# Raw weight loads with the gate sum's unit third, and the gate sum added by VectorE in pairs 3, 5 and 7

## The chip, the core and the metric

The kernel runs on one core of a Trainium2 chip. A core has a matrix engine (PE, with its weight loads shown as PEld), VectorE (DVE), ScalarE (ACT), GpSimd (POOL) and SyncE (SP), which run their own instruction streams and wait for one another by semaphores. SP and POOL here mostly issue DMAs; sixteen DMA engines carry them. The metric is the device time of one execution in microseconds (us), as a median of runs.

## The reference

A decoder trunk of two layers over 512 tokens with model width 1024, in float32. Each layer is a feed-forward block, a token mixing and a second feed-forward block; a last norm follows.

```python
def swiglu(h, w_gate, w_up, w_down):
    return (jax.nn.silu(h @ w_gate) * (h @ w_up)) @ w_down

for l in range(DEPTH):                      # DEPTH = 2, D_MODEL = 1024, D_FF = 2816
    x = x + 0.5 * swiglu(rms_norm(x, ffn1_norm[l]), ffn1_wg[l], ffn1_wu[l], ffn1_wd[l])
    h = rms_norm(x, mix_norm[l])
    z = h @ w_in[l]                         # q | k | v | conv_B | conv_C | conv_h
    ...                                     # sliding-window attention and a short convolution
    x = x + jnp.concatenate([attn_out, conv_out], axis=-1) @ w_out[l]
    x = x + 0.5 * swiglu(rms_norm(x, ffn2_norm[l]), ffn2_wg[l], ffn2_wu[l], ffn2_wd[l])
return rms_norm(x, final_norm)
```

Nearly all the work is in the weight products: four feed-forward blocks with gate, up and down weights, and two mixings with their input and output weights.

## The kernel before, in words

**Precision.** Each weight tile of 128 x 1024 is loaded raw (512 KB) and split in two: ScalarE casts it to a high part wh, VectorE subtracts to get the rest, wl (function `split`, line 228). PE then makes three products per piece: wh with the high part of the activations, wh with their low part, wl with the high part. Activations are split the same way. wh and wl have three buffers each, so a split can run at most about two groups ahead of PE; `take_split` asks for the split two places ahead (`SPLIT_AHEAD`).

**Seven products instead of eight.** Most weights are multiplied by a Winograd scheme on 2 x 2 quarters of the weights. With a11, a12, a21, a22 as quarters, the weight forms used are, in this order (`FORMS`): a11, a12, s2 = a11 + s1, s3 = a21 + a11, s1 = a21 + a22, a22, s4 = a12 + s2, signs left to the activations' side. This is called a seven here. In the gate and up weights, quarter rows are the two weights (gate quarters a11 and a12, up quarters a21 and a22) and s3 is the sum that the change calls the gate sum. Each form comes in two halves h of one 128 x 1024 tile, so a seven has 14 groups, and PE takes them one after another: seven steps of 24 products (line 837, or 822 in the mixing).

**Where sevens occur.** A feed-forward block runs its stages in the order of `INNER`: a plain stage and a down stage, then five pairs of gate and up blocks (`("w", b)` with b = 1, 3, 5, 7, 9), then two down-projection sevens (`("s", 1)` and `("s", 5)`), then a rest. The last block of the kernel ends with a stage of its own (`("e", 5)`) in place of the second down-projection seven. Each mixing has one seven for its output weights. That makes twenty sevens of pairs, four of `("s", 1)`, three of `("s", 5)` and two of the mixing. In the traces, tiles of the down-projection sevens end in `_s`, of the mixing in `_m`, of the last stage in `_e`.

**Raw loads.** `plan` lists the loads as units, two (h = 0 and 1) for each of five raw tiles of a seven: a11; s1, loaded as a21 with a22 accumulated onto it; a12; s3, loaded as a21 with a11 accumulated onto it; a22. `need_raw` issues the first load of a unit on SP's queue (line 210 for its DMA) and the second, where there is one, as an accumulating DMA on POOL's queue (line 223). An accumulating DMA waits until the plain load has landed. The raw tiles share eight buffers, so a load starts when an earlier tile has been released; SP's queue stands in the order of the units.

**In-place sums.** a11's tile becomes s2 when VectorE adds s1 to it (line 269), after a11 itself has been split. a12's tile becomes s4 when that s2 is added to it, once a12 has been split: by VectorE (line 291) or, in the sevens marked "share", by an accumulating DMA (line 289). a11 and s3 are released at form s3, s1 at its own form, a22 at its own, a12 at s4.

**What sets the order of work.** The instruction order on each engine comes from a planner that walks the program with its own estimates of durations: it takes the earliest instruction in program order that is ready by its clock. The order is fixed at build time; at run time each engine waits in that order. `tc.issue_after` adds edges by hand: in "share" sevens the s2 addition is placed behind the split just before it (`state["rest"]`). `last` in `need_split` and `LOAD_AHEAD` only say how far ahead in program order loads are requested.

Of the kernel before, what the change touches and what calls it, by code (L numbers as in the profile page):

```python
# [75 lines left out]
def trunk_kernel(  # L76
# [23 lines left out]
    nc = tc.nc  # L100
# [92 lines left out]
    units = []  # L193
    order = []
    raw_of, split_of = {}, {}
# [4 lines left out]
    def add_unit(*unit):  # L200
        units.append(unit)
        return len(units) - 1
# [24 lines left out]
    def split(hi, lo, raw, eng=nc.vector):  # L227
        return nc.scalar.copy(hi, raw), eng.tensor_sub(lo, raw, f32(hi))  # L228

    def split_far(hi, lo, raw):  # L230

        nc.scalar.activation(lo, raw, AF.Copy, scale=-1.0)
        nc.scalar.copy(hi, raw)
        return nc.gpsimd.dma_start(out=f32(lo), in_=raw, accum_op=ALU.add)

    def need_split(g):
        while state["split"] <= min(g, len(order) - 1):
            n = state["split"]
            u, what = order[n]
            far = what == "far"  # L240
            if what in (None, "far"):
                need_raw(u if far else max(u, min(u + LOAD_AHEAD, state["hold"] or len(units))))
                raw = raw_of.pop(u)
            elif isinstance(what, tuple) and what[0] == "end":

                _, what, h = what
                at = {"a11": 2, "s2": 2, "s3": 3, "s1": 3, "a12": 4, "a22": 5, "s4": 5}[what]
                need_raw(u + 3 * at + h + LOAD_AHEAD)
                raws = {name: u + 3 * i + h for i, name in enumerate(END_LOADS)}
                if what == "s2":  # L250
                    with tc.issue_after(state["rest"]):
                        nc.vector.tensor_add(raw_of[raws["a11"]], raw_of[raws["a11"]], raw_of[raws["s1"]])
                raw = raw_of[raws["a11" if what in ("s2", "s4") else what]]
            elif isinstance(what, tuple):

                what, h, how = what
                far = how == "far"
                last = {"a11": 0, "a12": 4, "s2": 2, "s3": 6, "s1": 2, "a22": 8, "s4": 4}[what]
                need_raw(u + h if far else u + max(last, 4) + h + LOAD_AHEAD)
                a11, s1, a12, s3, a22 = (raw_of.get(u + 2 * i + h) for i in range(5))  # L260
                if what == "s2":

                    late = state["late"] if h else None
                    if not state["late"] and how == "share":
                        late = state["rest"]
                    if how == "behind":
                        late = state["mark"]
                    with tc.issue_after(late) if late else nullcontext():
                        nc.vector.tensor_add(a11, a11, s1)  # L269
                raw = {"a11": a11, "a12": a12, "s2": a11, "s3": s3, "s1": s1, "a22": a22, "s4": a12}[what]  # L270
            shape = list(raw.shape)
            hi = wpool.tile(shape, F32R, tag="wh", bufs=3, name=f"wh_{n}")
            lo = wpool.tile(shape, F32R, tag="wl", bufs=3, name=f"wl_{n}")
            if far:
                sent = split_far(hi, lo, raw)
            else:
                state["cast"], state["rest"] = (i.ins for i in split(hi, lo, raw))
                if isinstance(order[n][1], tuple) and order[n][1][2] == "mark":
                    state["mark"] = state["rest"]
            if isinstance(order[n][1], tuple) and order[n][1][0] == "end":  # L280
                if what == "a12":
                    nc.gpsimd.dma_start(out=raw_of[raws["a11"]], in_=raw, accum_op=ALU.add)
                if what in ("s3", "s1", "a12", "a22"):
                    del raw_of[raws[what]]
                if what == "s4":
                    del raw_of[raws["a11"]]
            elif isinstance(order[n][1], tuple):
                if what == "s3" and how == "share":
                    nc.gpsimd.dma_start(out=a12, in_=a11, accum_op=ALU.add)
                elif what == "s3":  # L290
                    nc.vector.tensor_add(a12, a12, a11)
                done = {"s3": (0, 3), "s1": (1,), "a22": (4,), "s4": (2,)}.get(what, ())
                for i in done:
                    del raw_of[u + 2 * i + h]
            split_of[n] = (hi, lo)
            state["split"] += 1
            if far:

                with tc.issue_after(sent.ins):
                    need_raw(u + LOAD_AHEAD + (4 + h if isinstance(order[n][1], tuple) else 0))  # L300
# [26 lines left out]
    def abreast(kc):  # L327

        return max(1, KC // kc) if kc in (2, 4) else 1
# [34 lines left out]
    def plan():  # L364
        def cols(src, k0, kc, n, how=None, last=False):
            wide = abreast(kc)
            for b in halves_of(n, wide, last):
                order.append((add_unit((src, k0, kc, b * P, wide * P)), how))

        def plain(wg, wu, b):  # L370
            for w in (wg, wu):
                for j in range(2):
                    order.append((add_unit((w, 0, KC, (2 * b + j) * P, P)), None))

        def seven(at, how):


            u = len(units)
            for what in (((0, 0),), ((1, 0), (1, 1)), ((0, 1),), ((1, 0), (0, 0)), ((1, 1),)):
                for h in range(2):  # L380
                    add_unit(*(at(o, j, h) for o, j in what))
            order.extend((u, (what, h, how(what, h))) for what in FORMS for h in range(2))

        def ffn(wg, wu, wd, stages, near=False):
            for what, b in stages:
                how = "far" if b == (0,) and not near else None
                if what == "p":
                    plain(wg, wu, b)
                if what == "w":
                    seven(  # L390
                        lambda o, j, h: ((wg, wu)[o], KC // 2 * j + 2 * h, 2, 2 * b * P, S),
                        lambda what, h: "far"
                        if (b, what, h) == (1, "a11", 0)
                        else {("a12", 0): "mark", ("s2", 1): "behind"}.get((what, h))
                        if near and b == 3
                        else None,
                    )
                if what == "s":
                    seven(
                        lambda o, j, h: (wd, 2 * b + KC // 2 * j + 2 * h, 2, o * S, S),  # L400
                        lambda what, h: None if (b, what) == (1, "s3") else "share",
                    )
                if what == "d":
                    cols(wd, 2 * b[0], 2 * len(b), KC, how, len(b) == 2)
                    if len(b) == 2:
                        closing.append(len(units) - 1)
                if what == "e":
                    u = len(units)
                    roomy.update(range(u, u + 3))
                    for form_ in END_LOADS:  # L410
                        ojs = {"s1": ((1, 0), (1, 1)), "s3": ((1, 0), (0, 0))}
                        for i in range(3):
                            add_unit(
                                *(
                                    (wd, 2 * b + (KC + 2 * j if i == 2 else KC // 2 * j + 2 * i), 2, o * S, S)
                                    for o, j in ojs.get(form_, ((0, int(form_ == "a12")) if form_ != "a22" else (1, 1),))
                                )
                            )
                    order.extend((u, ("end", what, i)) for what in END_FORMS for i in range(3))

        for l in range(DEPTH):
            ffn(ffn1_wg[l], ffn1_wu[l], ffn1_wd[l], INNER, l == 0)
            for c in MIX_COLS:
                for j in range(2):
                    order.append((add_unit((w_in[l], 0, KC, (2 * c + j) * P, P)), None))
            seven(
                lambda o, j, h: (w_out[l], KC // 2 * j + 2 * h, 2, o * S, S),
                lambda what, h: "share",
            )
            ffn(ffn2_wg[l], ffn2_wu[l], ffn2_wd[l], INNER if l + 1 < DEPTH else LAST)  # L430
# [1349 lines left out]
```

## Time and profile before

| | |
|---|---|
| median of 3 runs | 1626.28 us (1625.93 to 1626.74) |
| profiled execution | 1626.23 us |
| its span, first to last instruction | 1624.4 us |
| PE busy | 1615.6 us, 7571 products |
| VectorE busy | 1376.8 us |
| ScalarE busy | 1177.8 us |
| POOL busy | 216.4 us |
| accumulating loads from wg, wu, wd, w_out | 40, 40, 34, 8 of 512 KB |
| granted PE clock | 1.0 throughout |

The profiled execution is one run of the program; its time is larger than its span by what lies outside the first and last instruction. Busy time of PE is counted from pipelined products whose ends are modelled, so the pace of product starts says more than the busy share. In the trace's rows a start and a duration in us come first, then engine, line, operation, tiles (written <- read), and in brackets the idle time before the instruction and what ended it. Rows of a queue (SPq) are issues of DMAs.

### The profile page before, as it was taken

Reading aid. Unit: us, or ns where it says so; the run is one execution under the profiler, and the core shown is the slowest. Engines: PE = TensorE matmul, PEld = TensorE weight load, DVE = VectorE, ACT = ScalarE, POOL = GpSimd, SP = SyncE. Lnnn points to the kernel's source line nnn. Section 1 sums busy time; section 2 is a strip of 40 time slices with the busy share of each in tenths; the row PEclk is TensorE's granted clock in tenths of the full one; section 3 lists DMA queues with packets and bytes.
Section 4 is the critical chain, followed back from the end, with each engine's and each line's share of the span. In section 5 each row is a group of like instructions: output and inputs, shape, how many; then the busy total and the mean of one; then the engine's idle time right before and its main releaser. Section 6 shows DMA issues by size and latency. Waiting matters only on the chain.

```text
span 1624.4 us, 21158 instructions
## 1 busy us (share of the span) xinstructions
PE 1615.6 (99%) x7571; PEld 1348.7 (83%) x7571; DVE 1376.8 (85%) x1788; ACT 1177.8 (73%) x1511; POOL 216.4 (13%) x191
## 2 busy tenths in 40 slices
PE   9999999999999999999999999999999999999998
PEld 7888888888898888888888888888888988888887
DVE  7978798988899877798998777989688998678997
ACT  6667777857766677778865777788586767878665
POOL 1211111001211111111011111110012111111121
PEclk9999999999999999999999999999999999999999
DMA  9999999823597699999767999998136978999892
GB/s 268 214 232 208 228 208 212 238 60 78 139 228 178 174 224 217 217 211 227 220 143 183 224 214 227 213 220 216 45 91 156 233 149 220 227 220 220 245 228 72
DMA packets 306030, 313.92 MB, mean 193 GB/s; under 512 B 125500, under 2 KB 188548, under 8 KB 305924
## 3 DMA queue, kind: packets, MB, share of 16 engines
q1 hardware_dynamic: 265412, 230.90, 50.0%
q0 software_dynamic: 40048, 81.27, 29.2%
q8 instruction: 59, 0.97, 0.2%
q10 hardware_dynamic: 464, 0.40, 0.1%
q14 instruction: 47, 0.39, 0.1%
HBM read 264.29 MB, written 2.10 MB: 164 GB/s over the span
## 4 chain that ended last, share of the span: by engine, by line
PE 96%; DVE 2%; ACT 1%; DMA 1%; issue 0%; SPq 0%; ACTq 0%; DVEq 0%
PE x L837 27%; PE y L837 13%; PE x_s L837 9%; PE acc L318 7%; PE w L837 7%; PE acc L319 7%; PE acc L321 7%; PE y_s L837 5%; PE x_m L822 3%; PE w_s L837 3%; PE y_m L822 1%; PE y_e L837 1%; PE x_e L837 1%; PE acc L699 1%; PE w_m L822 1%; DVE wl L228 1%
## 5 line engine op out<-in xcount | busy, mean ns | idle before, releaser
L228 DVE TENSOR_TENSOR wl<-raw,wh 128x1024 fp32r<-128x1024 f32 (+1 forms) x494 | 599.1, 1221 | 162.4 <-ACT wh L228 161.0
L228 ACT CAST wh<-raw 128x1024 fp32r<-128x1024 f32 (+1 forms) x494 | 513.7, 1043 | 303.9 <-PE x L837 92.9
L318 PE MATMUL acc<-xh,wh 128*128 128x512 f32 x392 | 153.3, 393 | 0.5 <-ACT wh L228 0.5
L319 PE MATMUL acc<-xl,wh 128*128 128x512 f32 x392 | 153.1, 391 | 0.0
L321 PE MATMUL acc<-xh,wl 128*128 128x512 f32 x384 | 149.6, 390 | 0.0
L223 POOL DMA_DIRECT2D raw<-in_ffn_wu_dram x40 | 50.6, 1277 | 380.6 <-DMA raw<-in_ffn_wu_dram 200.4
L318 PEld LDWEIGHTS acc<-xh,wh 128*128 128x128 f32 x392 | 73.8, 188 | 15.2 <-ACT wh L228 0.6
L319 PEld LDWEIGHTS acc<-xl,wh 128*128 128x128 f32 x392 | 73.7, 188 | 14.4
L321 PEld LDWEIGHTS acc<-xh,wl 128*128 128x128 f32 x384 | 72.1, 188 | 15.2
L223 POOL DMA_DIRECT2D raw<-in_ffn_wd_dram x34 | 41.0, 1218 | 272.9 <-DMA raw<-in_ffn_wd_dram 166.7
L223 POOL DMA_DIRECT2D raw<-in_ffn_wg_dram x40 | 49.0, 1232 | 205.2 <-DMA raw<-in_ffn_wu_dram 105.0
L269 DVE TENSOR_TENSOR raw<-raw,raw 128x1024 f32<-128x1024 f32 x58 | 70.5, 1220 | 3.2 <-DMA raw<-in_ffn_wu_dram 2.0
L1101 ACT COPY raw_a<-turned 128x1024 uint16<-128x1024 uint16 x48 | 63.5, 1357 | 0.0
L837 PE MATMUL x<-wl,ft1h 128*128 128x512 f32 x160 | 62.4, 390 | 0.0
L837 PE MATMUL w<-wh,fb21h 128*128 128x512 f32 x160 | 62.3, 390 | 0.0
L837 PE MATMUL y<-wh,ft3h 128*128 128x512 f32 x160 | 62.3, 390 | 0.0
L837 PE MATMUL x<-wl,ft2h 128*128 128x512 f32 x160 | 62.3, 389 | 0.0
L837 PE MATMUL x<-wh,ft1h 128*128 128x512 f32 x160 | 62.3, 389 | 0.0
L837 PE MATMUL x<-wh,ft2h 128*128 128x512 f32 x160 | 62.3, 389 | 0.0
L837 PE MATMUL x<-wh,ft1l 128*128 128x512 f32 x160 | 62.3, 389 | 0.0
L837 PE MATMUL x<-wh,ft2l 128*128 128x512 f32 x160 | 62.2, 389 | 0.0
L837 PE MATMUL w<-wh,fb21l 128*128 128x512 f32 x160 | 62.2, 389 | 0.0
(517 smaller groups left out, 4546.6 us busy)
## 6 DMA issues: line engine op xcount, KB each, us to landing
raw<-in_ffn_wu_dram SPq DMA_DIRECT2D x127, 512.0 KB, 5.4
raw<-in_ffn_wd_dram SPq DMA_DIRECT2D x105, 512.0 KB, 5.6
raw<-in_ffn_wg_dram SPq DMA_DIRECT2D x86, 512.0 KB, 5.2
raw<-in_ffn_wu_dram POOLq DMA_DIRECT2D x40, 512.0 KB, 9.0
raw<-in_ffn_wg_dram POOLq DMA_DIRECT2D x40, 512.0 KB, 6.2
raw<-in_w_in_dram SPq DMA_DIRECT2D x36, 512.0 KB, 4.0
raw<-in_ffn_wd_dram POOLq DMA_DIRECT2D x34, 512.0 KB, 8.4
raw<-in_w_out_dram SPq DMA_DIRECT2D x20, 512.0 KB, 4.1
```

The costliest lines, as they stand in the source:

```text
L223: nc.gpsimd.dma_start(out=r, in_=rows_of(*more), accum_op=ALU.add)
L228: return nc.scalar.copy(hi, raw), eng.tensor_sub(lo, raw, f32(hi))
L269: nc.vector.tensor_add(a11, a11, s1)
L318: nc.tensor.matmul(acc, hi[:, k, :], rhs[k][0], start=k == first, stop=False)
L319: nc.tensor.matmul(acc, hi[:, k, :], rhs[k][1], start=False, stop=False)
L321: nc.tensor.matmul(acc, lo[:, k, :], rhs[k][0], start=False, stop=k == last)
L699: nc.tensor.matmul(opening[n], (lo if part == "w" else hi)[:, k, :], xl if part == "x" else xh, start=n not in begun, stop=k == KC - 1 and ...
L822: nc.tensor.matmul(accs[c // 2][:, c % 2, :], w[:, k, cols], x_[:, 2 * h + k, :], start=start and c % 2 == 0 and h + k + i == 0, stop=h + ...
L837: nc.tensor.matmul(accs[u], x_[:, 2 * h + k, tok], w[:, k, :], start=start and h + k + i == 0, stop=h + k == 2 and i == 2, skip_group_chec ...
L1101: nc.scalar.copy(words(raws[self.b][:, c, :]), self.to[:, :, c, :])
```

## The change

The five raw tiles of a seven are loaded in the order a11, s1, s3, a12, a22 instead of a11, s1, a12, s3, a22. This holds for every seven built by `seven`: pairs, down-projection sevens and mixing outputs. The last stage of the kernel has its own order and is not touched. `last`, the indices in `need_split` and the releases follow the new places.

In the pairs with 1 < b < 9, that is b = 3, 5 and 7, the third unit is a21 alone, without an accumulating load. VectorE adds a11 to it in place (a 128 x 1024 addition), in program order right after the split of a12 and before a11 is overwritten by s2. That is two additions per pair, 24 in the kernel, and 24 accumulating loads from wg fewer.

```diff
-                last = {"a11": 0, "a12": 4, "s2": 2, "s3": 6, "s1": 2, "a22": 8, "s4": 4}[what]
+                last = {"a11": 0, "a12": 6, "s2": 2, "s3": 4, "s1": 2, "a22": 8, "s4": 6}[what]
                 need_raw(u + h if far else u + max(last, 4) + h + LOAD_AHEAD)
-                a11, s1, a12, s3, a22 = (raw_of.get(u + 2 * i + h) for i in range(5))
+                a11, s1, s3, a12, a22 = (raw_of.get(u + 2 * i + h) for i in range(5))
...
             elif isinstance(order[n][1], tuple):
+                if what == "a12" and len(units[u + 4 + h]) == 1:
+                    nc.vector.tensor_add(s3, s3, a11)
                 if what == "s3" and how == "share":
                     nc.gpsimd.dma_start(out=a12, in_=a11, accum_op=ALU.add)
                 elif what == "s3":
                     nc.vector.tensor_add(a12, a12, a11)
-                done = {"s3": (0, 3), "s1": (1,), "a22": (4,), "s4": (2,)}.get(what, ())
+                done = {"s3": (0, 2), "s1": (1,), "a22": (4,), "s4": (3,)}.get(what, ())
...
-        def seven(at, how):
+        def seven(at, how, here=False):
             u = len(units)
-            for what in (((0, 0),), ((1, 0), (1, 1)), ((0, 1),), ((1, 0), (0, 0)), ((1, 1),)):
+            s3 = ((1, 0),) if here else ((1, 0), (0, 0))
+            for what in (((0, 0),), ((1, 0), (1, 1)), s3, ((0, 1),), ((1, 1),)):
...
+                        here=1 < b < 9,
```

## The prediction

> **What bounds the kernel.** The page first: its span, the busy time by engine, the DMA engines' busy tenths in forty slices, and the head of the chain of work that ended last.
>
> ```profile
> span 1624.4 us, 21158 instructions
> PE 1615.6 (99%) x7571; PEld 1348.7 (83%) x7571; DVE 1376.8 (85%) x1788; ACT 1177.8 (73%) x1511; POOL 216.4 (13%) x191
> DMA  9999999823597699999767999998136978999892
> PE 96%; DVE 2%; ACT 1%; DMA 1%; issue 0%; SPq 0%; ACTq 0%; DVEq 0%
> ```
>
> PE is busy for all but 1624.4 - 1615.6 = 8.8 us. The waits of PE, and one piece of the merged chain, show how full it is inside:
>
> ```profile
> PE idle L151 <- DVE warm L646: 1.2, 1, 1.2
> PE acc L318 <- ACT wh L228: 0.5, 1, 0.5
> PE acc L699 <- ACT xh L470: 0.2, 1, 0.2
> ...
> 251.87 5.44 PE y_s L837 x24
> ```
>
> PE's waits come to 1.9 us together, and none is at line 837, where the pairs and the down-projection sevens multiply. A step of 24 products there takes 5.44 us, 0.227 us each. So the change has next to no wait to remove; it can only keep PE fed or starve it. The profiled execution took 1626.23 us, its span and 1.8 us around it; the median of the three runs is 1626.28. I count from 1626.2.
>
> What can starve PE is a late weight split (ScalarE's cast to wh, then VectorE's subtraction to wl), behind a raw load or behind an addition. So each edit is weighed by the room of the split that it delays.
>
> **The pairs 3, 5 and 7.** Four feed-forward blocks, three pairs, two halves: 24 additions come in and 24 accumulating loads go. First the nearest addition, the accumulating load on POOL and as a DMA (KB, us to landing), and busy times over one such pair (PE, PEld, DVE, ACT, POOL); then VectorE's rows around the second form of that pair, and PE's first use of its wl.
>
> ```profile
> L269 DVE TENSOR_TENSOR raw<-raw,raw 128x1024 f32<-128x1024 f32 x58 | 70.5, 1220 | 3.2 <-DMA raw<-in_ffn_wu_dram 2.0
> L223 POOL DMA_DIRECT2D raw<-in_ffn_wg_dram x40 | 49.0, 1232 | 205.2 <-DMA raw<-in_ffn_wu_dram 105.0
> ...
> raw<-in_ffn_wg_dram POOLq DMA_DIRECT2D x40, 512.0 KB, 6.2
> ...
> 603.00:641.00 38.00, 38.00 (x169) 31.45 (x169) 27.62 (x29) 28.03 (x33) 5.05 (x5) 1.00 0.94 222
> ```
>
> ```profile
> 594.60 1.23 DVE L228 TENSOR_TENSOR wl<-raw,wh 128x1024 fp32r<-128x1024 f32 x1 [1.49 <-ACT wh L228]
> 604.41 1.23 DVE L228 TENSOR_TENSOR wl<-raw,wh 128x1024 fp32r<-128x1024 f32 x1 [0.17 <-ACT wh L228]
> ...
> 607.60 0.39 PE L837 MATMUL w<-wl,fb21h 128*128 128x512 f32 x1
> ```
>
> An addition of this shape is 1.22 us, so VectorE gets 24 x 1.22 = 29.3 us more: 27.62 + 2.44 = 30.1 of 38.0 us in such a pair. On average that is covered. Locally VectorE is full from 594.60 to 604.41, and the split at 604.41 ends at 605.64, 1.96 us before PE wants it. Before 594.60 stand 1.49 us of idle time, enough for one addition if its raw quarters have landed and the planner puts it there. One addition inside the full stretch then takes 1.22 of the 1.96 us: nothing reaches PE. Both inside would take 2.44 - 0.17 = 2.27, which is 0.3 too much. What is queued behind an addition on VectorE is the s2 addition (it overwrites the a11 that the new one reads), then s2's cast on ScalarE and its split. The ends are 0 and 29.3 us (every addition on the path); a gain I leave to the rivals. I take 0.1 us per pair, 12 x 0.1 = 1.2 us, near the lower end because the quoted room covers one addition.
>
> The 24 accumulates took POOL 24 x 1.23 = 29.6 us and moved 12.6 MB. Nobody on the path waited for them, so I cost their removal at 0 us.
>
> **The load order, in every seven but the last one of the kernel.** SP's queue keeps its issue times, since these follow from raw buffers that come free; only the third and fourth pair of loads swap places. a12, the second form to be split, now comes as late as s3 came. On POOL's queue the s3 accumulates, where they remain, move ahead of the a12 landings. I work it in the first down-projection seven: SP's four loads (s, duration), two DMA answers for the loads that start at 226.94 and 230.35, POOL's accumulates, then the queues' traffic in 231 to 235 us (q1 is SP's loads, q0 the accumulates: packets, MB, share) and q1's in 235 to 238 us.
>
> ```profile
> 222.34 8.38 SPq L210 DMA_DIRECT2D raw<-in_ffn_wd_dram  x4
> ...
> raw<-in_ffn_wd_dram SPq DMA_DIRECT2D x1, 512.0 KB, 9.1
> ...
> raw<-in_ffn_wd_dram SPq DMA_DIRECT2D x1, 512.0 KB, 7.3
> ...
> 222.91 2.48 POOL L223 DMA_DIRECT2D raw<-in_ffn_wd_dram  x2 [23.24 <-DMA raw<-in_ffn_wd_dram]
> 236.62 1.21 POOL L223 DMA_DIRECT2D raw<-in_ffn_wd_dram  x1 [11.24 <-DMA raw<-in_ffn_wd_dram]
> ...
> q0 software_dynamic: 258, 0.50, 66.8%
> q1 hardware_dynamic: 295, 0.57, 41.9%
> ...
> q1 hardware_dynamic: 302, 0.57, 50.1%
> ```
>
> The second s3 load lands at 230.35 + 7.3 = 237.65; that becomes a12's time. It lands so early because the two s1 accumulates have ended by 235, and the last 0.57 MB go alone. Beside an accumulate the loads moved 0.57 MB in 4 us, 0.14 MB/us. After the change the third unit lands where a12 did, so POOL no longer waits until 236.62: its accumulate stands ready behind the s1 ones, and the last 0.57 MB take 4.0 us instead of the 1.6 that 235 to 237.65 less a microsecond of tail leaves. a12's second half lands 2.4 us later, at 240.05. ScalarE and VectorE now:
>
> ```profile
> 238.00 1.05 ACT L228 CAST wh<-raw 128x1024 fp32r<-128x1024 f32 x1 [0.23 <-PE x_s L837]
> ...
> 239.75 1.22 DVE L228 TENSOR_TENSOR wl<-raw,wh 128x1024 fp32r<-128x1024 f32 x1
> 240.88 1.22 DVE L269 TENSOR_TENSOR raw<-raw,raw 128x1024 f32<-128x1024 f32 x1
> 248.02 3.49 DVE L228 TENSOR_TENSOR wl<-raw,wh 128x1024 fp32r<-128x1024 f32 x3
> ...
> 249.37 0.43 PE L837 MATMUL x_s<-wl,ft2h_s 128*128 128x512 f32 x1
> ```
>
> The cast slips by 240.05 - 238.00 = 2.05 us. VectorE's split at 239.75 had 239.75 - 239.05 = 0.70 us of cover, so it slips by 1.35. Behind it, by the order written out for a "share" seven, stand L269, the cast of s2, its split, L269 and the second split of s2 at 248.02, which ends at 249.24, 0.13 us before PE wants it. Small gaps on that way may give 0.1 back: PE waits 1.35 - 0.13 - 0.1, about 1.1 us. The bounds are 0 (the loads keep their lone pace: 237.65 is before 238.00) and 2.0 (no cover). There are four such sevens, one in each block: 4.4 us.
>
> The second down-projection seven (three of them): its busy times (order as above), then the load that starts at 268.57, q1's traffic in 274 to 277 us, the cast and the splits:
>
> ```profile
> 273.47:311.56 38.09, 38.09 (x169) 31.51 (x168) 35.55 (x37) 29.20 (x30) 4.23 (x4) 1.00 0.79 188
> ...
> raw<-in_ffn_wd_dram SPq DMA_DIRECT2D x1, 512.0 KB, 8.0
> ...
> q1 hardware_dynamic: 183, 0.33, 28.9%
> ...
> 276.16 1.05 ACT L228 CAST wh<-raw 128x1024 fp32r<-128x1024 f32 x1 [0.39 <-PE x_s L837]
> ...
> 277.25 1.23 DVE L228 TENSOR_TENSOR wl<-raw,wh 128x1024 fp32r<-128x1024 f32 x1 [0.22 <-ACT wh L228]
> 299.91 2.36 DVE L228 TENSOR_TENSOR wl<-raw,wh 128x1024 fp32r<-128x1024 f32 x2
> ...
> 301.36 0.40 PE L837 MATMUL y_s<-wl,ft4h_s 128*128 128x512 f32 x1
> ```
>
> Landing 268.57 + 8.0 = 276.6, 0.4 after the cast's old start; sharing with the s3 accumulate adds 0.33 MB at 0.14 instead of 0.38 MB/us (0.57 MB in 1.5 us), 2.3 - 0.9 = 1.4 us. The split at 277.25 waits for its cast already, so all 1.8 us pass to VectorE, which is busy for 35.55 of 38.09 us here, up to the split of 299.91 and on; that one has 301.36 - 301.13 = 0.2 us of room. Gaps on the way give some back: 1.2 us (bounds 0 and 1.8), three times: 3.6 us.
>
> The other ten sevens are the first and last pairs and the mixing outputs. For a last pair, the second s3 load (started at 191.38), the two a12 casts, the second split and PE:
>
> ```profile
> raw<-in_ffn_wu_dram SPq DMA_DIRECT2D x1, 512.0 KB, 6.5
> ...
> 198.83 2.15 ACT L228 CAST wh<-raw 128x1024 fp32r<-128x1024 f32 x2
> ...
> 202.33 1.22 DVE L228 TENSOR_TENSOR wl<-raw,wh 128x1024 fp32r<-128x1024 f32 x1
> ```
>
> 191.38 + 6.5 + 2.4 = 200.3, 0.4 after the second cast's start at 199.9; that cast ended at 200.98, and its split began only at 202.33. The cover is 1.35 us, so I cost these ten at 0; where it is gone, at up to 0.5 us each.
>
> Sum: 1.2 + 4.4 + 3.6 = 9.2 us; 1626.2 + 9.2 = 1635.4.
>
> The Trainium skill (DMA: Bandwidth & Descriptors, "Anatomy of one DMA — SWDGE (gpsimd) path") fits a transfer as 2.0 us plus bytes/436e3, by which an estimate for 512 KB is 3.2 us and every load would be down before its cast: the sum would be 1.2 us. This trace disagrees where it is crowded: 7.3, 8.0 and 9.1 us above.
>
> **The rivals.** *The loads are hidden (same).* If the remaining accumulates do not slow the moved loads, a12 lands at 237.65 and 276.6, a late cast of 0.4 us at most, and the 1.96 us of room in the pairs covers the additions: 1626.2 + 0 to 1.2, so 1626.8. For it: no wait of PE at line 837 so far, although loads of 7 to 9 us occur. Against: the 0.13 and 0.2 us of room. It decides below 0.8 us of lateness at the first seven's cast. The fit of the Trainium skill named above would make this the outcome.
>
> *VectorE becomes the bound in the pairs (slower still).* If the planner puts both additions into the full stretch ahead of a12's splits, and a late third load holds VectorE's queue, up to 24 x 1.22 = 29.3 us go on the path: 1655.5. For it: 9.8 us of VectorE without a gap. Against: 1.49 us of idle time before it, 30.1 of 38.0 us.
>
> *Faster.* 12.6 MB less for the DMA engines, and VectorE no longer waits for s1's accumulates (the 2.0 us in L269's row). More than the 8.8 us outside PE's busy time cannot be had, and most of that is before the first and after the last product: if 4 us were had, 1622.
>
> **The numbers.** Forecast, some or all of the down-projection sevens starve PE: 0.62, own range 1630 to 1644. Loads hidden: 0.26. VectorE bound: 0.08. Faster: 0.04. About 0.2% (3.3 us) is what a measurement of this kernel can tell from no change: slower 0.62 + 0.08 = 0.70, same 0.26, faster 0.04. The range reaches down into the hidden case and up over 0 + 8 + 8 + 5 us of bounds (pairs, first sevens 4 x 2.0, second about 3 x 1.8, ten others at 0.5): 1626.2 to 1646; it leaves out the last two rivals and a sliver.
>
> **What would show it.** Right: PE waits or weight loads that wait at line 837 in the steps x_s (ft2) and y_s (ft4) of the down-projection sevens; the fourth pair of loads landing after 240 and 277; steps of 5.44 us grown to 6 or 7. The additions at 1.22 us, 24 of them, with VectorE at some 30 of 38 us in a pair and no PE wait there; 16 instead of 40 accumulates from wg. Wrong: PE steps all at 5.44 us (hidden), waits of PE in pairs 3, 5 and 7 (VectorE the bound), or a remaining accumulate that POOL still issues late.

## The result, and the profile after

The changed kernel takes 1675.38 us (median of 4 runs, 1671.32 to 1677.58) against 1626.45 (1625.93 to 1626.74) of the kernel before on the same chip: 1.0297 times as long, 95% interval 1.0284 to 1.0310. It is slower, as forecast, but by 48.9 us where 9.2 were forecast, and outside the range, which ended at 1646.0. The profiled execution took 1676.32 us, its span and 1.8 us around it.

The page of the kernel after: its span and busy times, the chain that ended last, VectorE's new addition and the accumulates from wg that remain.

```profile
span 1674.5 us, 21124 instructions
PE 1634.5 (98%) x7571; PEld 1348.6 (81%) x7571; DVE 1401.2 (84%) x1812; ACT 1175.7 (70%) x1511; POOL 186.9 (11%) x167
PE 70%; DVE 12%; DMA 9%; issue 4%; ACT 4%; SPq 0%; DVEq 0%; ACTq 0%; POOLq 0%
L289 DVE TENSOR_TENSOR raw<-raw,raw 128x1024 f32<-128x1024 f32 x24 | 29.4, 1224 | 41.4 <-issue 20.5
raw<-in_ffn_wg_dram POOLq DMA_DIRECT2D x16, 512.0 KB, 11.3
```

The 24 additions cost 1.22 us each, as forecast, and POOL is down by 29.5 us (216.4 to 186.9; 29.6 forecast). But the additions have 41.4 us of idle time before them, 1.7 us each, and the chain, which was PE for 96%, now goes through VectorE, the DMAs and ScalarE for 25% of the span. The waits (engine, tile, line, releaser: us in total, times, longest) say where:

```profile
DVE raw L289 <- issue: 20.5, 7, 4.5
DVE raw L289 <- DMA raw<-in_ffn_wu_dram: 19.1, 10, 6.0
PE x L841 <- DVE wl L228: 14.2, 13, 3.4
PE x_s L841 <- DVE wl L228: 7.3, 9, 1.5
PE w_s L841 <- ACT wh L228: 3.0, 2, 2.8
PE w_s L841 <- DVE wl L228: 2.5, 3, 1.6
PE x_m L826 <- DVE ft2l_m L228: 1.7, 2, 0.9
```

PE waits in the pairs (x, no suffix), in the down-projection sevens (`_s`) and in the mixing (`_m`). Before, there was no wait of PE at the line that multiplies in the pairs and the down-projection sevens (837 there, 841 here).

Waits alone leave out products that run slowly. So I measure a stage by its product starts: for each product of 512 columns, the time to the next start less 0.2267 us (5.44 us for 24, as before). The products of the mixing sevens have 256 columns, 48 in a step of 5.76 us, so there 0.12 us is taken off. Over all the sevens but the last stage of the kernel this gives 51.0 us after and 0.8 before; the difference, 50.2, is nearly that of the spans, 50.1. By stage (us; the last column is the difference of medians to the kernel before on the same chip):

| kernel | pairs 3, 5, 7 | first, last pairs | `("s", 1)` | `("s", 5)` | mixing | time against before |
|---|---|---|---|---|---|---|
| before | -0.1 | 0.3 | 0.4 | 0.0 | 0.2 | |
| after | 22.2 | 0.4 | 18.1 | 7.0 | 3.3 | +48.9 |
| order_only | 1.8 | 1.4 | 17.7 | 6.3 | 2.7 | +28.3 |
| add_only | 50.8 | 0.3 | 0.3 | 0.0 | 0.3 | +50.6 |
| pairs_only_b | 25.4 | 2.3 | 0.4 | 0.0 | 0.3 | +21.9 |
| pairs_dummy | 0.3 | 0.4 | 0.4 | 0.1 | 0.2 | +0.7 |
| pairs_pinned | 11.8 | 0.3 | 0.3 | 0.0 | 0.3 | +11.6 |
| pairs_own | 3.7 | 0.3 | 0.4 | 0.1 | 0.3 | +4.9 |
| pinned | 10.5 | 2.6 | 21.5 | 4.7 | 4.1 | +36.6 |
| order_no_s3acc | 0.5 | 0.6 | 8.2 | 0.6 | 0.3 | +11.5 |

The stage columns are of the one profiled execution, which for pairs_only_b (1654.47 us) and pinned (1669.35) was the slowest of four, some 6 us above the median, so there they add up to more than the last column.

So there are two losses of similar size. The forecast had 1.2 us for the first and 8.0 for the second.

**A loss in a pair.** Rows of the kernel after around the end of pair 5 in the third block: ScalarE's cast of the second s4 half, VectorE from the next addition on, the load of the next seven's second a21 half (issued at 974.40), and PE in the last step of pair 5.

```profile
977.50 1.06 ACT L228 CAST wh<-raw 128x1024 fp32r<-128x1024 f32 x1 [1.67 <-PE y L841]
...
984.57 1.23 DVE L289 TENSOR_TENSOR raw<-raw,raw 128x1024 f32<-128x1024 f32 x1 [6.00 <-DMA raw<-in_ffn_wu_dram]
985.72 1.22 DVE L228 TENSOR_TENSOR wl<-raw,wh 128x1024 fp32r<-128x1024 f32 x1
...
raw<-in_ffn_wu_dram SPq DMA_DIRECT2D x1, 512.0 KB, 10.0
...
983.20 0.39 PE L841 MATMUL x<-wh,fb22l 128*128 128x512 f32 x1
986.99 0.50 PE L841 MATMUL x<-wl,fb22h 128*128 128x512 f32 x1 [3.40 <-DVE wl L228]
```

The cast of the second s4 half ended at 978.56, so its split could have run then. But VectorE's order has the addition of the next seven ahead of it, and the addition waits 6.00 us for its load, which lands 10.0 us after 974.40. The split starts at 985.72, and PE, which wanted its wl after 983.20, starts its next product 3.79 us later instead of 0.227. The addition itself is not late for anybody: its s3 is needed some twenty microseconds later. What is late is the split queued behind it, of a seven that has nothing to do with it. The work of the addition alone would have done no harm here: from 978.57, when VectorE was free, 1.23 us of addition and 1.22 us of split end at 981.0, before 983.20.

The rows put half of these waits under `issue`, that is, under no releaser that the profile shows. They are waits for a load all the same. The longest of them, and the DMA answer for the load issued at 1431.47:

```profile
1440.79 1.23 DVE L289 TENSOR_TENSOR raw<-raw,raw 128x1024 f32<-128x1024 f32 x1 [4.55 <-issue]
...
raw<-in_ffn_wu_dram SPq DMA_DIRECT2D x1, 512.0 KB, 9.2
```

The load lands at 1440.7 and the addition starts 0.1 us later. Each of the 14 waits of more than 1 us before an addition in this kernel ends in this way, within 0.2 us of the landing of a load on SP's queue.

**A loss in a down-projection seven.** The same seven as in the prediction, the first `("s", 1)`: the seven's first product before and after; two DMA answers for the a12 loads that start at 232.72 and 236.12; POOL's first s3 accumulate; ScalarE's casts of a12; VectorE; PE.

```profile
235.31 0.39 PE L837 MATMUL x_s<-wh,fb11h_s 128*128 128x512 f32 x1
```

```profile
239.60 0.39 PE L841 MATMUL x_s<-wh,fb11h_s 128*128 128x512 f32 x1
...
raw<-in_ffn_wd_dram SPq DMA_DIRECT2D x1, 512.0 KB, 11.4
...
raw<-in_ffn_wd_dram SPq DMA_DIRECT2D x1, 512.0 KB, 12.1
...
234.53 1.20 POOL L223 DMA_DIRECT2D raw<-in_ffn_wd_dram  x1 [1.71 <-DMA raw<-in_ffn_wd_dram]
...
244.27 1.05 ACT L228 CAST wh<-raw 128x1024 fp32r<-128x1024 f32 x1 [5.23 <-DMA raw<-in_ffn_wd_dram]
248.31 1.04 ACT L228 CAST wh<-raw 128x1024 fp32r<-128x1024 f32 x1 [1.56 <-DMA raw<-in_ffn_wd_dram]
...
245.84 0.69 DVE L1033 TENSOR_TENSOR p<-p,gate 128x512 f32<-128x512 f32 x1 [3.34 <-ACT gate L1032]
257.46 3.49 DVE L228 TENSOR_TENSOR wl<-raw,wh 128x1024 fp32r<-128x1024 f32 x3
...
245.71 0.40 PE L841 MATMUL w_s<-wh,fb21l_s 128*128 128x512 f32 x1
247.72 0.56 PE L841 MATMUL w_s<-wl,fb21h_s 128*128 128x512 f32 x1 [1.62 <-DVE wl L228]
258.74 0.50 PE L841 MATMUL x_s<-wl,ft2h_s 128*128 128x512 f32 x1 [0.96 <-DVE wl L228]
```

The first a12 half, on its way from 232.72 beside the accumulate issued at 234.53, is cast at 244.27, 4.67 us after the seven's first product; before, that cast was at 235.28, 0.03 ahead of it. ScalarE's queue stands behind the cast for 5.23 us, and with it VectorE, which waits 3.34 us for a gate that ScalarE computes after it. PE pays twice, 2.1 us in the step of a12 (245.71 to 247.72, and a late start of the step) and 1.1 us at s2's second split (257.46, then 258.74). This seven loses 5.2 us in all; 1.4 us of that are seven products at half pace, of which more below.

### The profile page after: what moved, and what is told of

Same layout as the page of the kernel before. It is cut to its first block, busy times and chain, and to the rows that moved or that the text cites. A ratio compares the mean times of both kernels' runs of the same rounds, so it can differ in the third digit from the quotient of the medians.

```text
span 1674.5 us, 21124 instructions
## 1 busy us (share of the span) xinstructions
PE 1634.5 (98%) x7571; PEld 1348.6 (81%) x7571; DVE 1401.2 (84%) x1812; ACT 1175.7 (70%) x1511; POOL 186.9 (11%) x167
## 4 chain that ended last, share of the span: by engine, by line
PE 70%; DVE 12%; DMA 9%; issue 4%; ACT 4%; SPq 0%; DVEq 0%; ACTq 0%; POOLq 0%
PE x L841 17%; PE y L841 8%; PE acc L320 6%; PE acc L321 6%; PE acc L323 6%; PE w L841 6%; DVE wl L228 6%; PE x_s L841 5%; PE y_s L841 4%; DMA raw<-in_ffn_wd_dram 3%; DMA raw<-in_ffn_wu_dram 3%; PE x_m L826 2%; ACT wh L228 2%; PE y_m L826 1%; DVE raw L269 1%
## 5 line engine op out<-in xcount | busy, mean ns | idle before, releaser
L841 PE MATMUL x<-wl,fb22h 128*128 128x512 f32 x160 | 63.7, 398 | 10.6 <-DVE wl L228 10.6
L269 DVE TENSOR_TENSOR raw<-raw,raw 128x1024 f32<-128x1024 f32 x58 | 72.3, 1250 | 0.4
L841 PE MATMUL x<-wl,fb11h 128*128 128x512 f32 x160 | 63.2, 395 | 3.7 <-DVE wl L228 3.6
L289 DVE TENSOR_TENSOR raw<-raw,raw 128x1024 f32<-128x1024 f32 x24 | 29.4, 1224 | 41.4 <-issue 20.5
L841 PE MATMUL w<-wl,fb21h 128*128 128x512 f32 x160 | 63.0, 394 | 0.6
L841 PE MATMUL x<-wh,fb22h 128*128 128x512 f32 x160 | 62.8, 393 | 0.0
L841 PE MATMUL x<-wh,fb22l 128*128 128x512 f32 x160 | 62.8, 392 | 0.0
L841 PE MATMUL x<-wh,fb11h 128*128 128x512 f32 x160 | 62.4, 390 | 0.0
## 6 DMA issues: line engine op xcount, KB each, us to landing
raw<-in_ffn_wg_dram POOLq DMA_DIRECT2D x16, 512.0 KB, 11.3
```

Of the source, the lines that this page charges most:

```text
L289: nc.vector.tensor_add(s3, s3, a11)
L841: nc.tensor.matmul(accs[u], x_[:, 2 * h + k, tok], w[:, k, :], start=start and h + k + i == 0, stop=h + k == 2 and i == 2, skip_group_chec ...
```

## The experiments

**order_only** keeps every accumulate and takes the new order in all sevens.

```diff
-                        here=1 < b < 9,
+                        here=False,
```

> The new load order in every seven, but the third unit keeps its accumulating load in pairs 3, 5 and 7, and VectorE gets no new addition. Theory A (in the pairs it is the new addition that stalls: it stands at the head of VectorE's queue and waits for its raw load, with splits behind it; in the down-projection and mixing sevens it is the a12 load that lands late): the pairs' 22 us go, the other 28 us stay: about 1654. Rival B (the load order alone starves the pairs too, a12 being late there): 1670 to 1676. By the sizes of the recorded prediction: 1634.

Measured: 1654.5 us (1651.71 to 1656.2), ratio 1.0164 (1.0147 to 1.0181). The down-projection and mixing sevens lose 26.7 us, nearly what they lose after (28.4), and pairs 3, 5 and 7 lose 1.8. So that half of the loss belongs to the order of loads, not to the addition. The first `("s", 1)` seven loses 3.0 us here, most of it at s2 and none at a12, against 5.2 after.

**add_only** keeps the old order; in pairs 3, 5 and 7 a21 alone is loaded as the fourth unit and VectorE adds a11.

```diff
+                if what == "a12" and len(units[u + 6 + h]) == 1:
+                    nc.vector.tensor_add(s3, s3, a11)
...
-            for what in (((0, 0),), ((1, 0), (1, 1)), ((0, 1),), ((1, 0), (0, 0)), ((1, 1),)):
+            for what in (((0, 0),), ((1, 0), (1, 1)), ((0, 1),), ((1, 0),) if here else ((1, 0), (0, 0)), ((1, 1),)):
```

> The old load order everywhere; only the accumulating load of s3 in pairs 3, 5 and 7 is replaced by VectorE's addition, placed in program order as in the change. Theory A: the down-projection and mixing sevens are as before (0 us lost), the pairs lose as much as in the change or more, since the raw quarter now lands one place later while the planner still puts the addition early: 1645 to 1665. Rival C (the addition costs only its 1.22 us of VectorE time, 24 x 1.22 = 29 us mostly covered): 1626 to 1630.

Measured: 1676.81 us (1672.59 to 1678.15), ratio 1.0303 (1.0286 to 1.0319), above the 1645 to 1665 that were expected; the pairs alone lose 50.8 us. The additions wait even longer here, since a21 is loaded later. The groups row has 62.2 us of idle time before them:

```profile
L289 DVE TENSOR_TENSOR raw<-raw,raw 128x1024 f32<-128x1024 f32 x24 | 29.3, 1222 | 62.2 <-issue 42.5 <-DMA raw<-in_ffn_wu_dram 19.7
```

The new order is thus no mishap for the addition: it halves this loss. But it costs some 27 us elsewhere.

**pinned** is the whole change, with the addition held behind the a12 split that precedes it in program order.

```diff
-                    nc.vector.tensor_add(s3, s3, a11)
+                    with tc.issue_after(state["rest"]):
+                        nc.vector.tensor_add(s3, s3, a11)
```

> The whole change, and each new addition is ordered on VectorE behind the split of a12 that stands before it in the program, so that it can't stand earlier in the queue. Theory A: by then the raw quarter has landed, the pairs lose little (0 to 4 us, the two additions in a full stretch of VectorE), the other sevens still 28 us: 1654 to 1658. Rival C' (VectorE's amount of work is what stalls the pairs): as the change or worse, 1675 and more.

Measured: 1662.89 us (1662.64 to 1669.35), ratio 1.0231 (1.0211 to 1.0252). That is above the 1654 to 1658 expected: the pairs lose 10.5 instead of 22.2 us, where 0 to 4 had been expected, and the rest stays.

**pairs_only** was to take the new order and the addition in pairs 3, 5 and 7 alone, the old order elsewhere.

```diff
-                last = {"a11": 0, "a12": 6, "s2": 2, "s3": 4, "s1": 2, "a22": 8, "s4": 6}[what]
+                new = len(units[u + 4]) == 1 and units[u + 4][0][0] is not units[u][0][0]
+                at3, at12 = (4, 6) if new else (6, 4)
+                last = {"a11": 0, "a12": at12, "s2": 2, "s3": at3, "s1": 2, "a22": 8, "s4": at12}[what]
...
-            for what in (((0, 0),), ((1, 0), (1, 1)), s3, ((0, 1),), ((1, 1),)):
+            third = (s3, ((0, 1),)) if here else (((0, 1),), s3)
+            for what in (((0, 0),), ((1, 0), (1, 1)), *third, ((1, 1),)):
```

> The new load order and the additions in pairs 3, 5 and 7 alone; all other sevens keep the old order. Theory A: only the pairs lose, 22 us: about 1648. Rival D (the losses in the down-projection and mixing sevens follow from the pairs' delays, not from their own order): near 1675.

Measured: 1658.31 us (1651.36 to 1663.72), ratio 1.0191 (1.0161 to 1.0221). By a slip in my condition (`new`) the two mixing sevens took part: they used a12 and s3 in each other's place and added a11 to the wrong one, which changes their part of the computation, and lost 13.3 us. So this time says nothing of pairs alone. **pairs_only_b** is the same with the condition mended, so that it holds where the third unit has the rows of a11, in pairs 3, 5 and 7 alone:

> The new load order and the additions in pairs 3, 5 and 7 alone; the down-projection sevens, the mixing sevens and the first and last pairs keep the old order and their accumulating loads (in the kernel labelled pairs_only the mixing sevens took part by mistake). Theory A: the pairs lose 11 to 22 us, everything else nothing: 1638 to 1648. Rival D (the other sevens lose by the pairs' delays): above 1655.

Measured: 1648.42 us (1641.37 to 1654.47), ratio 1.0132 (1.0102 to 1.0163). With order_only it splits the change in two: 21.9 + 28.3 = 50.2 us, against 48.9 for both together. What is left in question is why the pairs lose.

**pairs_dummy** keeps the order, the loads and VectorE's extra work of pairs_only_b, but the instruction reads and writes only a11, so it never waits for the third load. a11 is missing from s3 in these pairs. The edit against pairs_only_b:

```diff
-                    nc.vector.tensor_add(s3, s3, a11)
+                    nc.vector.tensor_tensor(a11, a11, a11, op=ALU.max)
```

> As pairs_only_b, but in the place of each new addition VectorE takes the maximum of a11 with itself, the same shape and nearly the same place, which does not touch the third load (a11 is left out of s3 in these pairs). Theory A: the same VectorE work without the wait on the load costs 0 to 4 us: 1626 to 1630. Rival C' (the work itself): as pairs_only_b, 1638 to 1648.

Measured: 1627.14 us (1626.53 to 1628.13), ratio 1.0004 (0.9994 to 1.0013), no difference. Its group, and then that of pairs_only_b:

```profile
L291 DVE TENSOR_TENSOR raw<-raw 128x1024 f32<-128x1024 f32 x24 | 29.3, 1222 | 0.4
```

```profile
L291 DVE TENSOR_TENSOR raw<-raw,raw 128x1024 f32<-128x1024 f32 x24 | 29.4, 1224 | 43.8 <-issue 27.2 <-DMA raw<-in_ffn_wu_dram 15.0 <-DVE p L1029 1.4
```

The same 29.3 us of VectorE cost nothing, and taking the 24 accumulates away gains nothing: VectorE has room for this work in the pairs. But the expectation's "nearly the same place" doesn't hold. The maximum writes a11, so it stands behind a11's own split. The second one of pair 7 in the third block in pairs_dummy, whose first product starts at 962.48, and the second addition of the same pair in pairs_only_b, where it starts at 984.05:

```profile
963.18 1.22 DVE L291 TENSOR_TENSOR raw<-raw 128x1024 f32<-128x1024 f32 x1
```

```profile
979.20 1.23 DVE L291 TENSOR_TENSOR raw<-raw,raw 128x1024 f32<-128x1024 f32 x1 [4.29 <-DMA raw<-in_ffn_wu_dram]
```

The maximum stands 0.7 us behind the pair's first product, the addition 4.85 us ahead of it, with splits of the pair before queued behind it. So this run takes away the wait and the place together. That the 25.4 us come from the wait and not from the work, the rows of a loss above say for one case; the next two runs test it by moving the addition itself.

**pairs_pinned** and **pairs_own** move the addition. The first holds it behind the a12 split, as pinned does; the second behind the second a11 split of its own seven (edit against pairs_pinned):

```diff
+                if what == "a11" and new:
+                    state["own"] = state["rest"]
                 if what == "a12" and new:
-                    with tc.issue_after(state["rest"]):
+                    with tc.issue_after(state["own"]):
                         nc.vector.tensor_add(s3, s3, a11)
```

> As pairs_only_b, but each new addition is ordered on VectorE behind the split of a12 before it. Theory A (waiting at the head of VectorE's queue for the raw load is the loss): what is left is the work in a full stretch of VectorE, 0.3 to 0.7 us a pair, so 1630 to 1636. Rival C' (VectorE's amount of work): as pairs_only_b.

> As pairs_pinned (new order and VectorE's additions in pairs 3, 5 and 7 alone), but the addition is held behind the second a11 split of its own seven instead of behind its a12 split. It can no longer stand ahead of the splits of the seven before; inside its own seven the planner may put it where it likes. Theory (all of the loss of the pairs is splits of the seven before, queued behind an addition that waits for its load): the first addition goes into idle time between a11's and a12's splits, only one is left in the full stretch, and the pairs lose less than the 11.8 us of pairs_pinned: 1626.5 plus some 3 to 8 us, 1630 to 1634. Rival (each place ahead of the a12 splits is too early for the third load): an a12 split now stands behind an addition that waits, PE waits at the a12 step w, and the time is above pairs_pinned's 1638, up to pairs_only_b's 1648.

Measured: pairs_pinned 1638.08 us (1637.19 to 1638.96), ratio 1.0069 (1.0052 to 1.0086), where 1630 to 1636 was expected; pairs_own 1631.24 us (1629.43 to 1631.99), ratio 1.0030 (1.0019 to 1.0042), where 1630 to 1634 was expected. VectorE in pairs_pinned, and then in pairs_own, both in pair 5 of the first block (L292 and L294 are the additions, L271 the s2 sums):

```profile
609.74 0.69 DVE L1037 TENSOR_TENSOR p<-p,gate 128x512 f32<-128x512 f32 x1 [1.00 <-ACT gate L1036]
610.68 1.23 DVE L228 TENSOR_TENSOR wl<-raw,wh 128x1024 fp32r<-128x1024 f32 x1 [0.25 <-PE x L845]
611.82 1.22 DVE L292 TENSOR_TENSOR raw<-raw,raw 128x1024 f32<-128x1024 f32 x1
...
614.09 1.22 DVE L292 TENSOR_TENSOR raw<-raw,raw 128x1024 f32<-128x1024 f32 x1
615.23 2.36 DVE L271 TENSOR_TENSOR raw<-raw,raw 128x1024 f32<-128x1024 f32 x2
```

```profile
603.48 1.22 DVE L294 TENSOR_TENSOR raw<-raw,raw 128x1024 f32<-128x1024 f32 x1
...
605.21 1.22 DVE L294 TENSOR_TENSOR raw<-raw,raw 128x1024 f32<-128x1024 f32 x1
...
606.95 2.35 DVE L228 TENSOR_TENSOR wl<-raw,wh 128x1024 fp32r<-128x1024 f32 x2
609.22 2.35 DVE L271 TENSOR_TENSOR raw<-raw,raw 128x1024 f32<-128x1024 f32 x2
```

In pairs_pinned both additions stand in the full stretch, behind the a12 splits and after 1.25 us of idle time that nobody used, and a typical pair loses 0.7 us at s2. Pair 3 of the first block alone loses 4.2, with seven products at half pace behind its stalls. In pairs_own they fill the idle time ahead of the a12 splits. Nine of its twelve pairs lose less than 0.3 us; the other three lose 3.8 together. In both kernels VectorE never stands idle just before an addition. With the addition unchanged, moving it to where its load has landed thus takes away 21.7 of the 25.4 us (17.0 by the medians). So a place where the addition is almost free exists, inside its own seven; the kernel after has it ahead of the splits of the seven before.

**order_no_s3acc** takes the new order everywhere, has no additions, and leaves the s3 accumulates out of the down-projection and mixing sevens; a11 is missing from s3 there.

```diff
-                if what == "a12" and len(units[u + 4 + h]) == 1:
-                    nc.vector.tensor_add(s3, s3, a11)
...
-            s3 = ((1, 0),) if here else ((1, 0), (0, 0))
+            share = how("s2", 0) == "share"
+            s3 = ((1, 0),) if here or share else ((1, 0), (0, 0))
...
-                        here=1 < b < 9,
+                        here=False,
```

> The new load order in every seven, no new additions, and in the down-projection and mixing sevens the accumulating load of s3 is left out (a11 is missing from s3 there). order_only lost 26.6 us in these sevens by its trace. Theory E (a12 comes late because the s3 accumulate, now ahead of it, shares the DMA engines with its load): they lose 3 to 8 us, 1630 to 1637. Rival F (a12's later place in the queue alone is enough): 20 us or more stay, 1648 and up.

Measured: 1638.0 us (1635.94 to 1641.29), ratio 1.0072 (1.0057 to 1.0087). Those sevens lose 9.1 us, a little more than the 3 to 8 expected, instead of order_only's 26.7. The twin to compare with is order_only, which differs by these accumulates alone. The first `("s", 1)` seven in order_only, where its first product starts at 237.10: the two a12 loads (issued at 229.95 and 233.36) and the cast of the second half. Then the same here, with the first product, the loads issued at 230.37 and 233.77, and PE's one wait:

```profile
raw<-in_ffn_wd_dram SPq DMA_DIRECT2D x1, 512.0 KB, 9.5
...
raw<-in_ffn_wd_dram SPq DMA_DIRECT2D x1, 512.0 KB, 10.1
...
243.56 1.05 ACT L228 CAST wh<-raw 128x1024 fp32r<-128x1024 f32 x1 [1.55 <-DMA raw<-in_ffn_wd_dram]
```

```profile
237.25 0.39 PE L840 MATMUL x_s<-wh,fb11h_s 128*128 128x512 f32 x1
...
raw<-in_ffn_wd_dram SPq DMA_DIRECT2D x1, 512.0 KB, 9.1
...
raw<-in_ffn_wd_dram SPq DMA_DIRECT2D x1, 512.0 KB, 7.0
...
241.94 1.05 ACT L228 CAST wh<-raw 128x1024 fp32r<-128x1024 f32 x1
...
253.37 0.50 PE L840 MATMUL x_s<-wl,ft2h_s 128*128 128x512 f32 x1 [1.51 <-DVE wl L228]
```

The accumulate hardly touches the first half (9.5 against 9.1 us) and slows the second: 10.1 against 7.0 us, a landing 6.4 instead of 3.5 us and a cast 6.5 instead of 4.7 us behind the seven's first product. In the second and third block the second half of this seven takes 11.3 and 11.7 us with the accumulate, 6.6 and 7.8 without. So two thirds of the loss, 17.6 of 26.7 us, go with the accumulates, which share the DMA engines with a12's second half. That is 9.5 of the 17.7 us of the four `("s", 1)` sevens and nearly all of the loss in the `("s", 5)` and mixing sevens. The rest is the new order alone, nearly all of it in the four `("s", 1)` sevens: 2.2, 1.0, 2.7 and 2.3 us.

## Why the prediction was right and wrong

*Right.* The sign; that a12's second half lands later because an accumulate now runs beside it (2.4 us forecast, 6.4 - 3.5 = 2.9 between order_only and order_no_s3acc); that s2's splits then starve PE at ft2 in the `("s", 1)` sevens; the addition's 1.22 us; 24 and 16 as counts; that removing accumulates gives nothing back and that VectorE has room for the added work, which pairs_dummy shows with no loss at all.

*The pairs: 1.2 us forecast, 22.2 measured.* The step that failed is the place of the addition. I let it stand somewhere between 594.60 and 604.41, "if its raw quarters have landed and the planner puts it there", and priced only its duration. The planner put it ahead of the last splits of the seven before, and there it waits for its load. The second rival named the late third load that holds VectorE's queue, but priced it as 24 x 1.22 us of work and gave it 0.08. The price of such a wait isn't the instruction's duration but the load's lateness, up to 6.0 us a time. I also listed what is queued behind the addition from its own seven only. In a place where its load has landed, the price of 0.1 us a pair is near: nine of twelve pairs in pairs_own lose less than 0.3 us. The 0.3 us that I gave for both additions ahead of the a12 splits was not tested; in pairs_pinned, which has them behind these splits, a typical pair loses 0.7 us. The range had no room for any of this: its upper end counts 0 for the pairs, though I had put their own ends at 0 and 29.3 us. (It also counts 8 us for 3 x 1.8 = 5.4 us.)

*The `("s", 1)` sevens: 4 x 1.1 forecast; 5.2, 2.0, 3.2 and 7.7 measured.* At s2 (ft2) PE loses 1.1, 1.7, 2.3 and 1.1 us, near the forecast, but that is in part luck: by the forecast nothing would be lost there without the accumulate, and in order_no_s3acc these sevens still lose 8.2 us, 5.8 of it at ft2. The step that failed is "SP's queue keeps its issue times". In the first seven SP issues a12's halves 1.49 us later against the first product than it issued s3's (6.88 instead of 8.37 us ahead for the first half: 239.60 - 232.72, 235.31 - 226.94), and 1.2 to 1.5 us later in order_only and order_no_s3acc too; what holds it there I did not take apart.

What the forecast left out is the step of a12 itself, since I followed a12's second half only. Its first half takes the place of the load with 9.1 us, whose row stands in the prediction, and had less cover. In the kernel after its cast slips by 4.70 us against the first product, in these parts: 0.78 since that place landed at 236.06, after the old cast's start at 235.28, and 0.1 from landing to cast; 1.49 for the later issue; and 2.33 since the load takes 11.45 instead of 9.12 us (232.72 to 244.17, 226.94 to 236.06). The last part is not the accumulate's alone: order_only has the same accumulate and 9.5 us for this load, and no wait of PE at this step in the first two of these sevens. Why the load is slower with the additions in the kernel stays open. The last block loses most, 7.7 us: there a cast holds PE itself, the 2.8 us in the row of w_s behind ACT. In the first and the last of these sevens 1.4 us more are products at half pace.

*The `("s", 5)` sevens: 3 x 1.2 forecast; 1.3, 2.6 and 3.1 measured,* 0.6 in all without the accumulates. The cause was the right one and the bound of 1.8 us too low; and PE waits at ft2 and ft3, not at ft4, where I had looked for it. *The other ten sevens: 0 forecast,* at most 0.5 us each; the pairs among them lose 0.4 us in all, the two mixing sevens 1.6 and 1.7 us, which goes with the accumulates (0.3 in all without them).

*The rival that the loads are hidden* is refuted: the first seven's first a12 cast is 4.7 us late, where 0.8 was to decide. The Trainium skill (DMA: Bandwidth & Descriptors, "Anatomy of one DMA — SWDGE (gpsimd) path") states its fit for one DMA of the kind that GpSimd issues; taken for SP's loads, as the prediction did, it gives an estimate of 3.2 us for 512 KB. The two a12 loads took 11.4 and 12.1 us, so it is no duration for loads in a crowded stretch.

## What the runs showed of the hardware

After some stalls PE's products run at half pace for about 3 us. Windows of the kernel after (columns: us, busy us and count of PE, PEld, DVE, ACT, POOL, the granted clock, DMA share, GB/s): the stall of 245.71 and the stretch behind it; then the time behind the stall of 983.20; then a second such stretch, in the last block.

```profile
245.70:248.00 2.30, 0.68 (x3) 0.28 (x2) 2.16 (x3) 1.04 (x2) 0.00 (x0) 1.00 0.77 145
248.00:251.40 3.40, 3.40 (x9) 2.67 (x9) 2.82 (x3) 2.96 (x4) 0.00 (x0) 0.51 0.02 3
...
987.00:990.00 3.00, 3.00 (x12) 2.16 (x12) 3.00 (x5) 1.76 (x3) 0.00 (x0) 1.00 0.55 171
1576.00:1579.00 3.00, 3.00 (x8) 2.32 (x8) 3.00 (x5) 1.05 (x1) 0.00 (x0) 0.50 0.00 0
```

The granted clock is 0.51 there, and a product takes 0.427 instead of 0.227 us. The kernel after has some 20 such products, 20 x 0.2 = 4 us of its 50; add_only has some 40, 8 us. The length of a single stall does not decide it: the 2.0 us at 245.71 were followed by it, the 3.79 us at 983.20 were not (the row from 987.00). The Trainium skill (TensorE: Matmul & The Clock Gate, "Part 1: The HAM clock gate (the "warmup" mystery)") says that the array's clock falls to half after about one idle window of 3.4 us, rises again after about as long a busy one, and that this window runs free. The half clock and the length of the slow stretch agree with the trace. The stall of 2.0 us that was followed by it is shorter than the page's window. So a wait of PE can cost more than its own length, which no term of my sum had.

## What to carry to other kernels

When a change gives an in-order engine an instruction that needs a DMA, price the wait and not the work: find where the scheduler may put it, when its data lands, and which instructions of other stages then stand behind it. A twin that does the same work without touching the late data shows whether the work has room; look where the scheduler puts it, since its place may move too, and move the instruction itself to test the wait. When loads trade places, follow every load, first half and second, to its first reader with its own row, ask whether the queue still issues it when it did, and count an accumulate beside it as lost bandwidth.
